# Table sums of the adaptive norms moved from columns of TensorE to row sums on VectorE, with 22 of the jobs in the plain feed-forward

## The chip, the core and the metric

The kernel runs on one core of one Trainium2 chip. The metric is the device time of one execution in microseconds (us). Engines are named TensorE (PE in the rows; PEld is its weight load), VectorE (DVE), ScalarE (ACT), GpSimd (POOL) and SyncE (SP, whose queue issues the DMAs).

## What is computed

One inference step of a network of two layers over 640 tokens (512 latent tokens and 128 prompt tokens) with 1024 features. Each layer is a gated feed-forward at half weight, a block of attention and recurrent mixers, and a second gated feed-forward. In front of each of the three stands an RMS norm whose scale, shift and gate come from a condition vector. There are two conditions, one for each group of tokens:

```python
def modulate(x, shift, scale):
    return x * (1 + scale) + shift

def adaln_params(cond, w_ada, b_ada):
    m = jax.nn.silu(cond) @ w_ada + b_ada
    return jnp.split(m[:, None, :], N_MOD, axis=-1)

def swiglu(h, w1, w2):
    gate, up = jnp.split(h @ w1, 2, axis=-1)
    return (jax.nn.silu(gate) * up) @ w2
...
        mod_ctx = adaln_params(c_ctx[None, :], w_ada[l], b_ada[l])
        mod_lat = adaln_params(c, w_ada[l], b_ada[l])
```

`w_ada` is 1024 x 9216 in each layer, 37.7 MB in float32. Its product with the two condition vectors is cut into 18 jobs for each layer, 36 in all; one job makes 512 outputs for both conditions from 2 MB of the table.

## The kernel before

Activations are kept transposed, features on the 128 partitions and tokens along the row (two halves of 320). Every large product is done in three TensorE passes: a float32 operand is split into a high part (a copy on ScalarE) and a remainder (a subtraction on VectorE, or on GpSimd), by `split` (L76); the weights go through `load` and `parts` (L80, L86) with six buffers for raw tiles and four for split ones. `linear` and `products` (L96 to L118) issue the matmuls.

The stages in order are: a start (L1256 to L1267) that makes the tables of the first norm and the first sums of squares; layer 0's first feed-forward, which is **plain** (no sums of weight blocks, all 22 blocks of hidden units at 96 matmuls); layer 0's mixer; its second feed-forward; then layer 1's feed-forward, mixer and feed-forward. The last three feed-forwards are plain in three blocks and use a scheme with seven products of sums of quarter blocks in the other 19 (`block`, L335), with extra sums on VectorE and GpSimd. A feed-forward goes through four passes of 5, 5, 6 and 6 blocks; each pass ends with eight products with `w2` that are added into `x` (L198). The mixer ends in attention over eight heads (`mla`, L1169 on) and the output product with `wo` (L667 to L677).

A job of the tables is `adaln(l, i)` (L375). In the start it is eight loads of 256 KB and eight TensorE matmuls with the condition as the two weight columns (L387), a copy of the 2 x 512 result (L409), four transposes (L412) and an addition of the bias (L417). Elsewhere (L389 to L407) the eight tiles are scaled and summed on the engines with features of the input on the partitions: two first products on ScalarE (L396), fourteen multiply-adds of 128 x 512 on VectorE (L398), then each of the two sums is split (a copy on ScalarE, a subtraction on GpSimd, tile `adah`), four TensorE matmuls with columns of ones add over the partitions (L407), and L409, L412 and L417 follow as in the start. The table tiles (`adaw`) have three buffers here, twelve in the start.

`plan` (L434) cuts each job into five steps and gives each a weight; `fill(weight, ...)` (L425) is called in the loops (12.4 after a block, 0.9 times the pass's size after each `w2` product, 1.5 in attention, 2.3 after a `wo` product) and issues the steps that have come due; `flush` issues the rest. By this plan jobs 0 to 3 are in the start, 18 in layer 0's first feed-forward, 4 in its second, 5 in layer 1's first feed-forward and 5 in layer 1's mixer (its attention heads and `wo` products). Layer 0's mixer and layer 1's second feed-forward have none. Within this order a compile-time scheduler places each engine's instructions by priority and by its own estimate of when they are ready; on the chip each engine and each queue then runs in the order so fixed.

Of the kernel before, what the change touches and what calls it, by code (L numbers as in the profile page):

```python
# [16 lines left out]
KD = 8  # L17
# [26 lines left out]
class Net:  # L44
# [193 lines left out]
    def ffn(self, w1, w2, A, B, G, plain=PLAIN):  # L238


        nc = self.nc
        tt = nc.vector.tensor_tensor
        with self.pool("ffn") as fp, self.banks(L=6, G=2):
            self.adap = fp
            low = lambda tag, bufs: fp.tile([P, 2, 320], F32, tag=tag, name=self.nm(tag), bufs=bufs)
            first = [self.weight(w, KD, P) for w in (w1[0], w1[NJ])]
            h, sums = self.combos(fp, A, B, plain < NJ)
            j = 0
            for size in PASSES:
                mid = []  # L250
                for _ in range(size):
                    sg = low("sg", 2)
                    if j < plain:
                        for n, w in enumerate((w1[j], w1[NJ + j])):
                            w = first[n] if j == 0 else self.weight(w, KD, P)
                            for c in range(2):
                                p = self.pt("L")[:, :320]
                                self.products(p, w, h[c])
                                if n == 0:
                                    i1 = nc.scalar.activation(sg[:, c], p, AF.Silu)  # L260
                                else:
# [110 lines left out]
        return self.modnorm(_Bufs(pool, dict(hf=3)), A, B)  # L372


    def adaln(self, l, i, start=False):  # L375


        nc, a, mod = self.nc, self.a, self.mods[l]
        ap = self.adap
        ps = None  # L380
        if start:
            kind = "G"
            ps = self.pt(kind)
            for q in range(KD):
                raw = ap.tile([P, 512], F32, tag="adaw", name=self.nm("adaw"), bufs=12)
                nc.sync.dma_start(raw, a['wada'][l, i, q])
                nc.tensor.matmul(ps[:2, :], lhsT=self.cs[:, q, :], rhs=raw, start=(q == 0), stop=(q == KD - 1))  # L387
        else:
            acc = [ap.tile([P, 512], F32, tag=t, name=self.nm(t), bufs=1) for t in ("ada0", "ada1")]  # L389
            for q in range(KD):  # L390
                raw = ap.tile([P, 512], F32, tag="adaw", name=self.nm("adaw"), bufs=3)
                nc.sync.dma_start(raw, a['wada'][l, i, q])
# [8 lines left out]
            kind = "G" if "G" in self.psb else "T"  # L401
            ps = self.pt(kind)
            for g in range(2):
                hi, lo = (ap.tile([P, 512], F32R, tag="adah", name=self.nm("adah"), bufs=2) for _ in range(2))
                self.split(acc[g], hi, lo, True)
                for n, x in enumerate((hi, lo)):
                    nc.tensor.matmul(ps[:2, :], lhsT=self.sel[:, g, :], rhs=x, start=(g + n == 0), stop=(g + n == 2))  # L407
        row = ap.tile([2, 512], F32, tag="adah", name=self.nm("adarow"), bufs=2)
        nc.scalar.activation(row, ps[:2, :], AF.Copy)  # L409
        ps = self.pt(kind)  # L410
        for q in range(4):
            nc.tensor.transpose(ps[:, q * 2:q * 2 + 2], row[:, q * P:(q + 1) * P], self.ident[:2, :2])  # L412
        pv = ps[:, :8].rearrange("p (q c) -> p q c", c=2)
# [51 lines left out]
    def mixer(self, l, A, B, G):  # L465
# [8 lines left out]
            h = self.modnorm_in(mp, A, B)  # L474
        self.close_x()
        gp = self.gpool = self.enter("gdn")
        st = self.enter("stage")
        stage = lambda s=None: st.tile([P, T], F32, tag="stg", name=self.nm("stg"), bufs=3)

# [164 lines left out]
        self.mla(l, range(2), hook=lambda: list(t))  # L644
        self.leave()
        with self.pool("wo") as wp:
            self.adap = wp
            o = {}

            def osplit(i, f):  # L650
# [16 lines left out]
            with self.banks(L=6, G=2):  # L667
                order = (8, 9, 10, 11, 4, 5, 6, 7, 0, 1, 2, 3)
                for n in range(KD):
                    w = self.weight(a['wo'][l, n, :, 8:], 4, P) + self.weight(a['wo'][l, n, :, :8], 8, P)  # L670
                    w = w[:4] + w[8:] + w[4:8]
                    if n < KD - 1:
                        i = self.residual(n, w, [o[i] for i in order], G, True)
                        self.fill(2.3, i, i)
                    else:
                        self.flush()
                        self.closing([n], [w], [o[i] for i in order], G)  # L677

    def hp_open(self):
# [394 lines left out]
    def pv(self, blocks, vv, o, r0, c0, width):  # L1074
# [25 lines left out]
        return nc.scalar.activation(o[r0:r0 + 64, c0:c0 + width], po[r0:r0 + 64, :width], AF.Copy)  # L1100

    def swa(self, l):
        nc, att = self.nc, self.att
# [63 lines left out]
    def mla(self, l, heads, wp=None, osplit=None, hook=None):  # L1167
        nc, a, att = self.nc, self.a, self.att
        for head in heads:  # L1169
# [25 lines left out]
            for pair in range(2):  # L1195
                prs = [fin(n, 0, 2, 320) for n in (2 * pair, 2 * pair + 1)]
                blocks = [(s, [(prs[j], s * P, j) for j in range(2)]) for s in range(5)]
                i = self.pv(blocks, vv, ot, r0, pair * 256, 256)
            if wp:
                self.fill(1.5, i, i)  # L1200
# [19 lines left out]
    def body(self):  # L1220
# [14 lines left out]
        sel = ct("sel", [P, 2, 2])  # L1235
        nc.vector.memset(sel, 0.0)
        for g in range(2):
            nc.vector.memset(sel[:, g, g:g + 1], 1.0)
        self.sel = ct("selr", [P, 2, 2], F32R)
        self.hi(self.sel, sel)  # L1240
# [13 lines left out]
        self.hp_open()  # L1254
        self.open_x()
        with self.pool("ada") as self.adap, self.banks(G=2, N=1):  # L1256
            for i in (0, 2, 1, 3):
# [27 lines left out]
        self.bd = [ct(f"bd{i}", [P, 512]) for i in range(4)]  # L1285
        for b in self.bd:
            nc.gpsimd.memset(b, 0.0)
# [4 lines left out]
        ffn, mix = 22 * 12.4 + 0.9 * 165, 6 * 1.5 + 7 * 2.3  # L1292
        for l in range(L):
            mods = lambda j: (self.A[l][j], self.mods[l][:, 3 * j], self.G[l][j])
            if l == 0:
                self.plan((jobs[4:6], 58), (jobs[6:22], ffn - 58))
            else:
                self.plan((jobs[26:31], ffn))
            self.ffn(a['w1a'][l], a['w2a'][l], *mods(0), NJ if l == 0 else PLAIN)
            self.plan((((), jobs[31:36])[l], mix))  # L1300
            self.mixer(l, *mods(1))
            self.plan(((jobs[22:26], ())[l], ffn))
            self.ffn(a['w1b'][l], a['w2b'][l], *mods(2))
        with self.pool("fin") as fp, self.banks(G=4):
            for j, p in enumerate((self.r[0], self.spread(self.r[1], 1, WINDOWS[1]))):
# [64 lines left out]
def _layout(x):  # L1370
# [22 lines left out]
    out['wada'] = C(x['w_ada'].reshape(L, KD, P, 18, 512).transpose(0, 3, 1, 2, 4))  # L1393
# [40 lines left out]
```

## Time and profile before

| | us |
|---|---|
| median of 3 runs | 3305.92 (3305.45 to 3310.22) |
| the profiled execution | 3302.95 |
| its span, first to last instruction | 3301.2 |
| mean granted TensorE clock | 0.979 of full speed |
| busy: TensorE, VectorE, ScalarE, GpSimd | 3182.5, 2383.2, 1559.5, 985.9 |

The span is what the profile covers; the execution's own time is 1.75 us more. Busy times are unions, so overlapping matmuls count once. A row of a group of instructions gives line, engine, operation, output and input tiles, shapes, count, busy time, mean duration, and the engine's idle time in front of them with what ended it. The "chain" is the sequence of work that is followed back from the last instruction of a stretch.

### The profile page before, as it was taken

The page shows a single profiled execution, that of the slowest core. Times are in us where ns is not written, and L with a number is a line of the kernel's source. Part 1 is how long each engine was busy: PE and PEld are TensorE (multiplying, and loading weights), DVE is VectorE, ACT ScalarE, POOL GpSimd, SP SyncE. Part 2 cuts the span into 40 slices and gives each one's busy share as a digit, 9 for nine tenths or more (in the row PEclk, how much of TensorE's full clock was granted, in tenths as well). Part 3 has the DMA queues.
Part 4 walks back from the last instruction along what each step waited for, and adds up shares of the span by engine and source line. Part 5 has one row for each costly group of instructions (what it writes and reads, how often), then busy time and mean ns, then how long its engine had stood idle before and what let it go on. Part 6 is the DMA issues. An engine that isn't in the chain of part 4 may idle for free.

```text
span 3301.2 us, 58370 instructions
## 1 busy us (share of the span) xinstructions
PE 3182.5 (96%) x21400; PEld 3053.1 (92%) x21400; DVE 2383.2 (72%) x5137; ACT 1559.5 (47%) x3453; POOL 985.9 (30%) x846
## 2 busy tenths in 40 slices
PE   8999999999998999999999999999998989899998
PEld 5999999999987899999999999999997869899998
DVE  4767767787886447887877897777778656766875
ACT  3333334645666544433453343465466664533433
POOL 0111101221343303553434464222114331233541
PEclk9999998999999999999999999999999989999999
DMA  6445544332534322333223333323244255222222
GB/s 221 144 140 164 158 142 139 96 99 85 171 90 115 97 75 90 97 102 106 89 85 100 106 98 101 117 86 110 73 158 123 69 150 157 77 74 84 77 90 68
DMA packets 234352, 364.90 MB, mean 111 GB/s; under 512 B 34129, under 2 KB 82385, under 8 KB 234065
## 3 DMA queue, kind: packets, MB, share of 16 engines
q1 hardware_dynamic: 234064, 361.17, 35.6%
q8 instruction: 168, 2.75, 0.3%
q14 instruction: 120, 0.98, 0.1%
HBM read 315.03 MB, written 46.04 MB: 109 GB/s over the span
## 4 chain that ended last, share of the span: by engine, by line
PE 79%; DVE 9%; ACT 4%; issue 3%; DMA 2%; POOL 2%; SPq 0%; POOLq 0%; ACTq 0%; DVEq 0%
PE psL L114 35%; PE psL L101 29%; PE psT L1098 3%; PE psG L859 2%; DVE wlo L78 2%; PE psT L1087 1%; PE psS L1192 1%; PE psS L898 1%; DVE ada L398 1%; PE psS L901 1%; PE psG L407 1%; DMA of<-do 1%; PE psS L1137 1%; DMA adaw<-in_wada_dram 1%; ACT pr L1066 1%
## 5 line engine op out<-in xcount | busy, mean ns | idle before, releaser
L69 ACT ACTIVATE whi<-wr 128x512 fp32r<-128x512 f32 (+3 forms) x733 | 417.7, 578 | 680.6 <-PE psL L114 407.3
L114 PE MATMUL psL<-mid,whi 128*128 128x320 f32 x2816 | 629.9, 311 | 0.0
L78 DVE TENSOR_TENSOR wlo<-wr,whi 128x512 fp32r<-128x512 f32 (+2 forms) x619 | 428.6, 699 | 244.6 <-ACT whi L69 243.4
L114 PEld LDWEIGHTS psL<-mid,whi 128*128 128x128 f32 x2816 | 474.7, 189 | 4.1 <-issue 0.5
L114 PE MATMUL psL<-mid,wlo 128*128 128x320 f32 x1408 | 435.2, 310 | 1.0 <-DVE wlo L78 1.0
L398 DVE SCALAR_TENSOR_TENSOR ada<-adaw,cs,ada 128x512 f32<-128x512 f32 x448 | 341.3, 794 | 24.3 <-ACT ada L396 17.5
L101 PE MATMUL psL<-hx,whi 128*128 128x320 f32 x1368 | 339.7, 310 | 0.0
L198 DVE SCALAR_TENSOR_TENSOR x<-psL,G,x 128x320 f32<-128x320 f32 (+2 forms) x432 | 173.1, 435 | 167.1 <-PE psL L114 166.5
L78 POOL TENSOR_TENSOR adah<-ada,adah 128x512 fp32r<-128x512 f32 x64 | 94.7, 1480 | 648.1 <-ACT adah L69 507.1
L114 PEld LDWEIGHTS psL<-mid,wlo 128*128 128x128 f32 x1408 | 265.3, 189 | 2.8 <-DVE wlo L78 1.3
L78 DVE TENSOR_TENSOR wlo<-ws,whi 128x512 fp32r<-128x512 f32 x228 | 241.0, 1060 | 29.2 <-ACT whi L69 28.4
L101 PE MATMUL psL<-ha,whi 128*128 128x320 f32 x952 | 237.0, 317 | 9.8 <-DVE ha L309 8.5
L101 PEld LDWEIGHTS psL<-hx,whi 128*128 128x128 f32 x1368 | 239.3, 188 | 0.6
L101 PE MATMUL psL<-hc,whi 128*128 128x320 f32 x952 | 236.6, 310 | 3.0 <-ACT hc L308 3.0
L101 PE MATMUL psL<-hb,whi 128*128 128x320 f32 x952 | 230.8, 310 | 0.0
L101 PE MATMUL psL<-hd,whi 128*128 128x320 f32 x808 | 229.4, 310 | 0.0
L1071 POOL TENSOR_TENSOR pr<-pr,den 128x640 f32<-128x640 f32 (+3 forms) x160 | 153.8, 968 | 231.1 <-DVE den L1070 173.7
L69 ACT ACTIVATE whi<-ws 128x512 fp32r<-128x512 f32 x228 | 142.1, 628 | 164.5 <-PE psL L101 123.5
L101 PE MATMUL psL<-hx,wlo 128*128 128x320 f32 x684 | 212.1, 310 | 0.0
L352 POOL TENSOR_TENSOR ws<-wr,wr 128x512 f32<-128x512 f32 x57 | 84.6, 1484 | 389.9 <-DMA wr<-in_w1b_dram 185.8
L78 POOL TENSOR_TENSOR wlo<-wr,whi 128x512 fp32r<-128x512 f32 x114 | 167.3, 1477 | 81.6 <-ACT whi L69 61.7
L1098 PE MATMUL psT<-pt,vv 128*128 128x256 f32 (+1 forms) x640 | 163.4, 381 | 17.2 <-ACT pt L1094 16.5
(361 smaller groups left out, 8355.9 us busy)
## 6 DMA issues: line engine op xcount, KB each, us to landing
adaw<-in_wada_dram SPq DMA_DIRECT2D x288, 256.0 KB, 2.8
wr<-in_w1a_dram SPq DMA_DIRECT2D x176, 256.0 KB, 2.9
wr<-in_w1b_dram SPq DMA_DIRECT2D x176, 256.0 KB, 2.9
wr<-in_win_dram SPq DMA_DIRECT2D x108, 256.0 KB, 2.8
wr<-in_w2a_dram SPq DMA_DIRECT2D x64, 256.0 KB, 2.7
wr<-in_w2b_dram SPq DMA_DIRECT2D x64, 256.0 KB, 2.7
wr<-in_wo_dram SPq DMA_DIRECT2D x48, 256.0 KB, 2.8
dqn<-hd SPq DMA_DIRECT2D x24, 320.0 KB, 2.3
```

The lines of the kernel that those rows point to most:

```text
L69: self.nc.scalar.activation(dst, src, AF.Copy)
L78: (self.nc.gpsimd if gpsimd else self.nc.vector).tensor_tensor(lo, src, hi.bitcast(F32), ALU.subtract)
L101: self.nc.tensor.matmul(p, lhsT=w, rhs=r, start=(first and k + n == 0), stop=(last and k == kt - 1 and n == 2))
L114: i = nc.tensor.matmul(p[:m, :cw], lhsT=w[:, :m], rhs=r[:, c0:c0 + cw], start=(k == 0 and n == 0), stop=(k == kt - 1 and n == 2))
L198: i = self.nc.vector.scalar_tensor_tensor(xs, ps[j][:, c0:c0 + n], G[:, k, g:g + 1], xs, ALU.mult, ALU.add)
L352: pt(s1, a21, a22, ALU.add)
L398: nc.vector.scalar_tensor_tensor(acc[g], raw, c, acc[g], ALU.mult, ALU.add)
L407: nc.tensor.matmul(ps[:2, :], lhsT=self.sel[:, g, :], rhs=x, start=(g + n == 0), stop=(g + n == 2))
L859: nc.tensor.matmul(p[:, s], lhsT=lhs[:, s], rhs=rhs[:, s], start=True, stop=True)
L898: nc.tensor.matmul(p1[:, :P], lhsT=qw[:, u, c, 64 * d:64 * d + P], rhs=S, start=True, stop=True)
L1071: nc.gpsimd.tensor_tensor(pr, pr, den[:, 0:1].to_broadcast([P, w]), ALU.mult)
L1098: nc.tensor.matmul(po[:, oc:oc + w], lhsT=vv[:, vb, :], rhs=hl[ti][:, s0:s0 + w], start=(n == 0), stop=(n == len(place) - 1))
```

## The change

A job outside the first two (0 and 2, which stay on TensorE) now takes the table transposed: 128 output features on the partitions and the 1024 input features along the row. For each of four tiles of 128 x 1024 (512 KB, two buffers) and each condition, one VectorE instruction multiplies the tile with the condition (SiLU applied, copied to all partitions, tile `crow`, 1 MB) and writes the row's sum through `accum_out`. The sum already has the features on partitions, so the split, the matmuls with ones, the copy and the transposes fall away. `conditions` loads `crow` and applies SiLU on ScalarE, once in the start and once in each feed-forward that has jobs.

```diff
+            if self.job:
+                self.conditions()
...
+    def conditions(self):
+
+        self.crow = self.adap.tile([P, 2, D], F32, tag="crow", name=self.nm("crow"), bufs=1)
+        self.nc.sync.dma_start(self.crow, self.a['crow'].unsqueeze(0).to_broadcast([P, 2, D]))
+        for g in range(2):
+            self.nc.scalar.activation(self.crow[:, g], self.crow[:, g], AF.Silu)
+
...
-            acc = [ap.tile([P, 512], F32, tag=t, name=self.nm(t), bufs=1) for t in ("ada0", "ada1")]
-            for q in range(KD):
-                raw = ap.tile([P, 512], F32, tag="adaw", name=self.nm("adaw"), bufs=3)
-                nc.sync.dma_start(raw, a['wada'][l, i, q])
+            pv = ap.tile([P, 4, 2], F32, tag="adac", name=self.nm("adac"), bufs=2)
+            for q in range(4):
+                raw = ap.tile([P, D], F32, tag="adat", name=self.nm("adat"), bufs=2)
+                nc.sync.dma_start(raw, a['wadat'][l, i * 4 + q])
                 for g in range(2):
-                    c = self.cs[:, q, g:g + 1]
-                    if q == 0:
-                        nc.scalar.activation(acc[g], raw, AF.Copy, scale=c)
-                    else:
-                        nc.vector.scalar_tensor_tensor(acc[g], raw, c, acc[g], ALU.mult, ALU.add)
-                if q % 2:
-                    yield
...
+                    out = raw if g else ap.tile([P, D], BF16, tag="adas", name=self.nm("adas"), bufs=1)
+                    nc.vector.scalar_tensor_tensor(out, raw, 1.0, self.crow[:, g], ALU.mult, ALU.mult, accum_out=pv[:, q, g:g + 1])
+                yield
```

The plan changes too: 22 jobs in layer 0's first feed-forward, 5 in its second, 5 in layer 1's first, none in a mixer, and in the start jobs 1 and 3 take the new way.

```diff
             for i in (0, 2, 1, 3):
-                list(self.adaln(0, i, start=True))
+                list(self.adaln(0, i, start=i % 2 == 0))
...
-                self.plan((jobs[4:6], 58), (jobs[6:22], ffn - 58))
+                self.plan((jobs[4:6], 58), (jobs[6:26], ffn - 58))
             else:
-                self.plan((jobs[26:31], ffn))
+                self.plan((jobs[31:], ffn))
             self.ffn(a['w1a'][l], a['w2a'][l], *mods(0), NJ if l == 0 else PLAIN)
-            self.plan((((), jobs[31:36])[l], mix))
             self.mixer(l, *mods(1))
-            self.plan(((jobs[22:26], ())[l], ffn))
+            self.plan(((jobs[26:31], ())[l], ffn))
```

The calls of `fill` and `flush` in the mixer are removed. The four zeroed tiles `bd` of the recurrent mixer, made once before (L1285), are now made and zeroed at the start of each mixer, and the columns of ones (`sel`) are gone.

## Rows read from the trace of the kernel before

**Rows 1.** The page: busy time by engine, and the chain that ended last
```profile
PE 3182.5 (96%) x21400; PEld 3053.1 (92%) x21400; DVE 2383.2 (72%) x5137; ACT 1559.5 (47%) x3453; POOL 985.9 (30%) x846
PE 79%; DVE 9%; ACT 4%; issue 3%; DMA 2%; POOL 2%; SPq 0%; POOLq 0%; ACTq 0%; DVEq 0%
```

**Rows 2.** Timeline, ScalarE: the norm row that closes each feed-forward and mixer
```profile
551.80 0.44 ACT L227 ACTIVATE rn<-psG 128x320 f32<-128x320 f32 x1 [0.64 <-PE psG L163]
...
1220.55 0.44 ACT L227 ACTIVATE rn<-psG 128x320 f32<-128x320 f32 x1 [1.31 <-PE psG L163]
...
1677.93 0.44 ACT L227 ACTIVATE rn<-psG 128x320 f32<-128x320 f32 x1 [0.39 <-PE psG L163]
...
2144.27 0.44 ACT L227 ACTIVATE rn<-psG 128x320 f32<-128x320 f32 x1 [1.11 <-PE psG L163]
...
2839.58 0.44 ACT L227 ACTIVATE rn<-psG 128x320 f32<-128x320 f32 x1 [2.36 <-PE psG L163]
...
3285.54 0.44 ACT L227 ACTIVATE rn<-psG 128x320 f32<-128x320 f32 x1 [0.40 <-PE psG L163]
```

**Rows 3.** Busy time by stretch: length, then busy time and count of each engine
```profile
core 0: us, PE busy (x) PEld busy (x) DVE busy (x) ACT busy (x) POOL busy (x), PEclk, DMA share, GB/s
...
63.00:545.00 482.00, 479.83 (x3237) 467.50 (x3235) 339.85 (x592) 174.46 (x318) 53.21 (x36) 1.00 0.50 152
...
1216.00:1241.00 25.00, 20.23 (x125) 19.14 (x123) 21.52 (x56) 21.14 (x52) 3.93 (x4) 0.86 0.19 64
...
1700.00:2136.00 436.00, 428.64 (x2869) 420.39 (x2868) 357.39 (x561) 179.17 (x342) 195.02 (x130) 1.00 0.34 105
```

**Rows 4.** The chain by line in 63 to 545 us, the plain feed-forward
```profile
by line: PE psL L101 62.7%; PE psL L114 32.0%; PE psG L407 3.4%; PE psG L412 1.3%; POOL adah L78 0.3%; ACT adah L69 0.1%; ACT adarow L409 0.1%; issue 0.1%; ACTq L69 0.0%
```

**Rows 5.** Groups by line and shape: VectorE's multiply-adds, a one-column instruction, ScalarE's accumulator read
```profile
L398 DVE SCALAR_TENSOR_TENSOR ada<-adaw,cs,ada 128x512 f32<-128x512 f32 x252 | 182.8, 755 | 21.2 <-ACT ada L396 17.5 <-DMA adaw<-in_wada_dram 3.4
...
L307 DVE SCALAR_TENSOR_TENSOR mid<-x,A,rn 128x320 f32<-128x320 f32 x32 | 15.1, 547 | 0.0
...
L1070 DVE RECIPROCAL den<-den 128x1 f32<-128x1 f32 x160 | 25.4, 159 | 48.2 <-ACT pr L1066 46.8
...
L1066 ACT ACTIVATION_READ_ACCUMULATOR pr<-psS,nb,rq 128x1 f32 x80 | 16.2, 202 | 0.0
```

**Rows 6.** Timeline of VectorE at 147 us: two multiply-adds in a row
```profile
147.31 1.41 DVE L398 SCALAR_TENSOR_TENSOR ada<-adaw,cs,ada 128x512 f32<-128x512 f32 x2
```

**Rows 7.** Busy time of line 398 alone in two later stretches
```profile
1241.00:1680.00 439.00, 43.13 (x56) 1.00 0.31 96
1700.00:2136.00 436.00, 64.66 (x70) 1.00 0.34 105
```

**Rows 8.** The chain by line in layer 1's mixer: attention, 2640 to 2740, and `wo`
```profile
by line: PE psT L1098 24.7%; PE psS L1192 12.4%; PE psT L1087 10.6%; DMA of<-do 8.9%; issue 8.3%; DVE ada L398 5.8%; POOL pr L1071 5.8%; DVE mx L1061 4.2%; DMA adaw<-in_wada_dram 3.7%; ACT pr L1066 3.4%; ACT pt L1094 2.8%; POOL adah L78 2.5
...
by line: PE psL L114 86.3%; PE psG L407 3.4%; PE psG L145 2.8%; POOL adah L78 2.7%; PE psG L412 1.5%; ACT adah L69 1.3%; issue 0.8%; PE psT L1098 0.7%; ACT adarow L409 0.6%; ACT whi L69 0.1%; POOLq L78 0.0%; ACTq L69 0.0%
```

**Rows 9.** The start: timeline of VectorE and TensorE, and DMA to 60 us
```profile
44.80 0.17 DVE L417 TENSOR_TENSOR mod<-psG,small 128x8 f32<-128x8 f32 x1 [7.26 <-PE psG L412]
...
50.82 0.64 PE L101 MATMUL psL<-hc,whi 128*128 128x320 f32 x1 [2.98 <-ACT hc L308]
...
17.28 4.46 SPq L386 DMA_DIRECT2D adaw<-in_wada_dram  x6
...
GB/s 0 66 284 351 366 354 396 400 397 388 393 394 398 394 392 385 389 321 319 361 380 386 376 391 392 388 388 351 368 175 7 5 0 0 0 0 0 0 0 0
...
adaw<-in_wada_dram SPq DMA_DIRECT2D x35, 256.0 KB, 5.4
```

**Rows 10.** DMA in 63 to 545 us: issues, KB, us to landing; SP's waits
```profile
adaw<-in_wada_dram SPq DMA_DIRECT2D x141, 256.0 KB, 2.8
...
dx<-x SPq DMA_DIRECT2D x6, 320.0 KB, 3.5
...
SPq L392 <- DVE ada L398: 102.0, 107, 2.1
```

**Rows 11.** GpSimd's zeroing of the `bd` tiles
```profile
L1287 POOL MEMSET bd<- x4: 524/524/524, 0.7 to 2.1; 128x512 f32 x4
```

More of the change, by code (lines that the diff above doesn't have):

```diff
@@ L379, in adaln @@
         ap = self.adap
-        ps = None
         if start:
-            kind = "G"
-            ps = self.pt(kind)
+            ps = self.pt("G")
             for q in range(KD):
                 raw = ap.tile([P, 512], F32, tag="adaw", name=self.nm("adaw"), bufs=12)
-                nc.sync.dma_start(raw, a['wada'][l, i, q])
+                nc.sync.dma_start(raw, a['wada'][i // 2, q])
                 nc.tensor.matmul(ps[:2, :], lhsT=self.cs[:, q, :], rhs=raw, start=(q == 0), stop=(q == KD - 1))
-        else:
-            acc = [ap.tile([P, 512], F32, tag=t, name=self.nm(t), bufs=1) for t in ("ada0", "ada1")]
-            for q in range(KD):
-                raw = ap.tile([P, 512], F32, tag="adaw", name=self.nm("adaw"), bufs=3)
-                nc.sync.dma_start(raw, a['wada'][l, i, q])
+            row = ap.tile([2, 512], F32, tag="adarow", name=self.nm("adarow"), bufs=1)
@@ new lines, in adaln @@
+            nc.scalar.activation(row, ps[:2, :], AF.Copy)
+            ps = self.pt("G")
+            for q in range(4):
+                nc.tensor.transpose(ps[:, q * 2:q * 2 + 2], row[:, q * P:(q + 1) * P], self.ident[:2, :2])
+            pv = ps[:, :8].rearrange("p (q c) -> p q c", c=2)
+        else:
+            pv = ap.tile([P, 4, 2], F32, tag="adac", name=self.nm("adac"), bufs=2)
+            for q in range(4):
+                raw = ap.tile([P, D], F32, tag="adat", name=self.nm("adat"), bufs=2)
+                nc.sync.dma_start(raw, a['wadat'][l, i * 4 + q])
@@ L393, in adaln @@
                 for g in range(2):
-                    c = self.cs[:, q, g:g + 1]
-                    if q == 0:
-                        nc.scalar.activation(acc[g], raw, AF.Copy, scale=c)
-                    else:
-                        nc.vector.scalar_tensor_tensor(acc[g], raw, c, acc[g], ALU.mult, ALU.add)
-                if q % 2:
-                    yield
[L401 to L413, printed above, removed]
+                    out = raw if g else ap.tile([P, D], BF16, tag="adas", name=self.nm("adas"), bufs=1)
+                    nc.vector.scalar_tensor_tensor(out, raw, 1.0, self.crow[:, g], ALU.mult, ALU.mult, accum_out=pv[:, q, g:g + 1])
@@ L476, in mixer @@
         gp = self.gpool = self.enter("gdn")
+        self.bd = [gp.tile([P, 512], F32, name=self.nm("bd")) for i in range(4)]
+        for b in self.bd:
+            nc.gpsimd.memset(b, 0.0)
         st = self.enter("stage")
@@ L646, in mixer @@
         with self.pool("wo") as wp:
-            self.adap = wp
             o = {}
@@ L672, in mixer @@
                     if n < KD - 1:
-                        i = self.residual(n, w, [o[i] for i in order], G, True)
-                        self.fill(2.3, i, i)
+                        self.residual(n, w, [o[i] for i in order], G, True)
                     else:
-                        self.flush()
                         self.closing([n], [w], [o[i] for i in order], G)
@@ L1099, in pv @@
                              start=(n == 0), stop=(n == len(place) - 1))
-        return nc.scalar.activation(o[r0:r0 + 64, c0:c0 + width], po[r0:r0 + 64, :width], AF.Copy)
+        nc.scalar.activation(o[r0:r0 + 64, c0:c0 + width], po[r0:r0 + 64, :width], AF.Copy)
     def swa(self, l):
@@ L1197, in mla @@
                 blocks = [(s, [(prs[j], s * P, j) for j in range(2)]) for s in range(5)]
-                i = self.pv(blocks, vv, ot, r0, pair * 256, 256)
-            if wp:
-                self.fill(1.5, i, i)
+                self.pv(blocks, vv, ot, r0, pair * 256, 256)
             self.pv([(5, [(fin(4, T, 1, P), 0, 0)])], vv, ot, r0, TL, P)
@@ L1234, in body @@
         nc.vector.memset(self.ones, 1.0)
[L1235 to L1240, printed above, removed]
         self.mhalf = ct("mhalf", [P, 8])
@@ L1256, in body @@
         with self.pool("ada") as self.adap, self.banks(G=2, N=1):
+            self.conditions()
             for i in (0, 2, 1, 3):
-                list(self.adaln(0, i, start=True))
+                list(self.adaln(0, i, start=i % 2 == 0))
                 if i == 2:
@@ L1284, in body @@
         self.sh8 = [i ^ 8 for i in range(32)]
-        self.bd = [ct(f"bd{i}", [P, 512]) for i in range(4)]
-        for b in self.bd:
-            nc.gpsimd.memset(b, 0.0)
         self.nsink = ct("nsink", [P, 2 * 8])
@@ L1291, in body @@
         jobs = [(l, i) for l in range(L) for i in range(18)]
-        ffn, mix = 22 * 12.4 + 0.9 * 165, 6 * 1.5 + 7 * 2.3
+        ffn = 22 * 12.4 + 0.9 * 165
         for l in range(L):
@@ L1392, in _layout @@
     out['wo'] = tiles(x['w_out'], 12, P)
-    out['wada'] = C(x['w_ada'].reshape(L, KD, P, 18, 512).transpose(0, 3, 1, 2, 4))
+    out['wada'] = C(x['w_ada'][0].reshape(KD, P, 18, 512).transpose(2, 0, 1, 3)[0:4:2])
+    out['wadat'] = C(x['w_ada'].transpose(0, 2, 1).reshape(L, 72, P, D))
+    out['crow'] = C(np.stack([x['c'][0], x['c_ctx']]))
     fp = lambda v: v.reshape(L, -1, P).transpose(0, 2, 1)
```

## The prediction

> **What bounds the kernel now.** First the page: TensorE is busy for 96% of the span and holds 79% of the chain that ended last, VectorE holds 9% [rows 1]. So an edit pays where it takes TensorE work off the chain or ends a wait of TensorE, and costs where VectorE comes late. A mean over stages with different limits says no more than that, so next come the stages. The norm row that closes each of them marks its end [rows 2]: layer 0's mixer lasts 1220.55 - 551.80 = 668.8 us, its second feed-forward 457.4, layer 1's first feed-forward 466.3, its mixer 695.3, its second feed-forward 446.0. The last three feed-forwards do the same products, with 4, 5 and 0 jobs of the tables in them; the mixers are alike too, with 0 and 5. These differences are the price of the jobs as they stand: 11.4 us for 4, 20.4 for 5, and 26.5 for the 5 in the mixer.
>
> In the plain feed-forward, 63 to 545 us, TensorE is busy for 479.83 of 482 us and VectorE for 339.85, or 71% [rows 3]. Its chain is TensorE almost throughout, and the parts that belong to the tables (L407, L412, and waits for `adah` and `adarow`) are 3.4 + 1.3 + 0.3 + 0.1 + 0.1 = 5.2% [rows 4], or 25.1 us for 18 jobs: 1.4 us a job.
>
> **The change, part by part.** *TensorE's share of a job.* The four matmuls with ones, the transposes and the waits for their operands vanish. At 1.4 us a job this is 25.1 us in the plain feed-forward, whose added jobs then cost TensorE nothing, 5.6 us in layer 0's second feed-forward and 7.0 in layer 1's first.
>
> *VectorE's share.* Fourteen instructions of 755 ns go [rows 5]. Eight of 128 x 1024 come. From 320 columns at 547 ns to 512 at 755 a column costs 1.08 ns, so 1024 should take 755 + 512 x 1.08 = 1.31 us. Two in a row take 1.41 us, 0.05 each less than alone [rows 6], so 1.26. No VectorE row of this kernel has an accumulator output. On ScalarE, reading the accumulator is an instruction of its own, of 202 ns, and VectorE's one-column instruction takes 159 [rows 5]. The bounds are 0 and 0.20 us; I take 0.12, the one-column row less some overlap. A sum is then about 1.38 us and a job 11.0 us of VectorE, against 182.8 / 18 = 10.2 now. On VectorE the new way is thus no cheaper at all.
>
> The Trainium skill ("VectorE: DVE Perf Modes", "Two Vector instructions with no wait between them") says that a VectorE operation which also writes out its accumulator is two instructions, the main one and an accumulator read, and this speaks against the change. The same page's fit for float32 pairs, (N + 151)/0.96 ns, under "The TRN2 errata", gives an estimate of 1.22 us for the main one; with it a job would be 10.7 us. No run shown here has such a VectorE instruction.
>
> *22 jobs for 18 in the plain feed-forward.* Its other VectorE work is 339.85 - 182.8 = 157 us; the jobs become 22 x 11.0 = 242. That is 399 us in a stretch of 457 (482 less 25), or 87%. The bounds of what the crowding costs: nothing, as the chain shows at 71%; or what layer 1's first feed-forward pays at 357.39 of 436 us, 82% [rows 3], where 20.4 - 7.0 = 13.4 us are waits. Those blocks depend more on VectorE than the plain ones, so I take 8 us. Net -17.
>
> *Layer 0's second feed-forward, 5 jobs for 4.* TensorE -5.6. The waits (11.4 - 5.6 = 5.8 us) stay and grow with VectorE's job time, from 43.13 us [rows 7] to 55 or more: +2. The condition row needs two SiLUs of 1024 columns on ScalarE; they come ahead of the norm's work in a changeover where ScalarE is busy for 21.14 of 25 us [rows 3], so up to 2.4 us of them shows: +1.6. Net -2. *Layer 1's first feed-forward, 5 for 5.* TensorE -7.0; VectorE 64.66 us [rows 7] against some 60; ScalarE and GpSimd lose their part, -3 of the waits; the SiLUs +2. Net -8.
>
> *Layer 1's mixer.* All five jobs leave. If it becomes like layer 0's, 26.5 us go. The chain bears it out: in attention, `ada`, `adaw` and `adah` together hold 5.8 + 3.7 + 2.5 = 12% of 100 us, and in `wo` the tables hold 3.4 + 2.7 + 1.5 + 1.3 + 0.6 = 9.5% of 95 us [rows 8]: 21 us named, the rest in issue and queues. I take -26. The four memsets of 524 ns in each mixer [rows 11] run on GpSimd while the input products begin and nothing needs it: 0; uncovered, 2 us each.
>
> *The start.* The loads run near 390 GB/s until 44 us [rows 9]; `crow` adds 1 MB, 2.7 us. Jobs 1 and 3 now wait on VectorE. Their loads begin to be issued at 17.3 us [rows 9]; with `crow` ahead and 5.4 us to land, the first sum starts near 25, and sixteen of them end at 47 if none waits. With two buffers each of the last six loads can be issued only when a tile is done: (5.4 + 2.8) / 2 = 4.1 us a tile against 2.8 of work, up to 8 us more. The bounds are therefore +2 and +10 on the last table addition, now at 44.80, behind which the steady products start at 50.82 [rows 9]. I take +8, as the queue is full there.
>
> **Sum**: -17 - 2 - 8 - 26 + 8 = -45 us against the profiled execution's 3302.95: 3258. The median of the runs is 3.0 us above that execution, so 3261.
>
> **The rivals.** *The cover holds.* VectorE's added work fits into its idle time, GpSimd's and ScalarE's relief shortens more waits in the two later feed-forwards, and the start loses 3 us: -25 - 5 - 12 - 26 + 3 = -65, or 3241. For it: 47 us of VectorE's 142 idle us in the plain feed-forward would be enough. Against it: 87% leaves little play for a queue in fixed order.
>
> *VectorE becomes the bound in the plain feed-forward.* If a sum takes 1.65 us, 157 + 22 x 8 x 1.65 = 447 us of 457: the 25 us are given back whole, and the later feed-forwards gain nothing: -26 + 8 = -18, or 3288. For it: the accumulator's price is not in these rows. Against it: the read would have to take 0.39 us, three times my term and twice ScalarE's.
>
> *Slower: the table loads hold up VectorE's queue.* With two buffers the load of a tile is issued only when the tile two before is done. A load of 256 KB lands in 2.8 us, one of 320 KB in 3.5 [rows 10]; 512 KB should take 3.5 to 5.6. If steps run back to back, the 2.8 us of the tile between cover only part, and VectorE stands for w us in front of each of the 88 tiles, with the weight remainders and sums of the products behind it. The plain feed-forward then takes 399 + 88 w. The other stages give 28 us, so from w = (482 + 28 - 399) / 88 = 1.26 us the kernel is slower; at 1.5 it takes 3303 + 21 + 3 = 3327. For it: `fill` issues three or four steps at once, and SP already waits 102 us for VectorE to free table tiles [rows 10]. Against it: on average a tile has 457 / 88 = 5.2 us, and now VectorE waits only 3.4 us for `adaw` in this stretch [rows 5].
>
> *The mixer's 26.5 us are not the jobs'.* If only the `wo` part goes, it is 13 less: 3274.
>
> **How the numbers follow.** Forecast (3247 to 3274) 0.47; cover holds (3226 to 3247) 0.20; VectorE the bound (3274 to 3299) 0.17; mixer 0.07; loads hold the queue (3299 and more) 0.09. A measurement of this kernel tells about 0.2%, 6.6 us, from no change. Slower by more than that needs w above 1.3 us: 0.07. Within it: 0.06, the edges of the two unfavourable cases. Faster: 0.87. The range leaves out the slow case and the lowest end: 3228 to 3296.
>
> **What would show it.** Right: no psG matmul in 63 to 545; that stretch's products in about 465 us with VectorE near 87%; layer 1's mixer within 3 us of layer 0's; rows of the sums near 1.26 us with an accumulator read of about 0.12 to 0.2; the first steady product at 55 to 61 us. Wrong: VectorE waiting for `adat` by more than 0.7 us a tile; a sum above 1.6 us; TensorE waiting for VectorE's weight remainders (L78) in the plain feed-forward by more than 20 us; a mixer that stays near 695.

## The result and the profile after

The changed kernel takes 3233.56 us (median of 4 runs, 3228.27 to 3235.18) against 3305.68 before (4 runs): a ratio of 0.9784, 95% interval 0.9769 to 0.9799, or 72 us less. The forecast was 3261, its range 3228 to 3296, and the rival "the cover holds" stood at 3241. The direction, the range and the main mechanism were right; the gain is 1.6 times the one forecast, near the lower edge of the range, and nearer to that rival.

The page's busy times and the shares of its last chain, after (answering to [rows 1]):

```profile
PE 3102.4 (96%) x21104; PEld 3006.9 (93%) x21104; DVE 2389.2 (74%) x5230; ACT 1471.1 (45%) x3297; POOL 902.6 (28%) x786
PE 74%; DVE 14%; ACT 4%; issue 4%; DMA 3%; POOL 1%; SPq 0%; POOLq 0%; DVEq 0%; ACTq 0%
```

TensorE, ScalarE and GpSimd lose 80, 88 and 83 us of work. VectorE gains 6: two more jobs are on it, and a job's sums have become hardly cheaper there, but all that stood around them is gone. VectorE's share of the chain has grown from 9% to 14%.

The norm row that closes each stage, after (answering to [rows 2]):

```profile
533.24 0.44 ACT L227 ACTIVATE rn<-psG 128x320 f32<-128x320 f32 x1 [1.48 <-PE psG L163]
...
1197.80 0.44 ACT L227 ACTIVATE rn<-psG 128x320 f32<-128x320 f32 x1 [1.31 <-PE psG L163]
...
1654.38 0.44 ACT L227 ACTIVATE rn<-psG 128x320 f32<-128x320 f32 x1 [0.39 <-PE psG L163]
...
2109.16 0.44 ACT L227 ACTIVATE rn<-psG 128x320 f32<-128x320 f32 x1 [0.39 <-PE psG L163]
...
2772.88 0.44 ACT L227 ACTIVATE rn<-psG 128x320 f32<-128x320 f32 x1 [1.31 <-PE psG L163]
...
3218.12 0.44 ACT L227 ACTIVATE rn<-psG 128x320 f32<-128x320 f32 x1 [0.39 <-PE psG L163]
```

The differences of these marks, and the first product from which TensorE runs on steadily (50.82 us before, 63.01 after), divide the 67.8 us by which the profiled span is shorter:

| stretch | before | after | change | forecast |
|---|---|---|---|---|
| start, to the first steady product | 50.8 | 63.0 | +12.2 | +8 |
| plain feed-forward, layer 0 | 501.0 | 470.2 | -30.8 | -17 |
| mixer, layer 0 | 668.8 | 664.6 | -4.2 | 0 |
| second feed-forward, layer 0 | 457.4 | 456.6 | -0.8 | -2 |
| first feed-forward, layer 1 | 466.3 | 454.8 | -11.6 | -8 |
| mixer, layer 1 | 695.3 | 663.7 | -31.6 | -26 |
| the rest | 461.6 | 460.5 | -1.1 | 0 |

The new sums (line 408), their accumulator reads, and VectorE's waits for their tiles, over the whole kernel:

```profile
L408 DVE SCALAR_TENSOR_TENSOR adas<-adat,crow x136: 1207/1217/2209, 27.0 to 2086.8; 128x1024 bf16<-128x1024 f32 x136
L408 DVE DVE_READ_ACCUMULATOR adas<-adat,crow x136: 74/81/86, 28.1 to 2087.9; 128x1 f32 x136
...
  DMA adat<-in_wadat_dram: 11.8, 18
...
DMA to landing us min/median/max: 3.3/3.7/7.6
```
```profile
26.99 1.23 DVE L408 SCALAR_TENSOR_TENSOR adas<-adat,crow 128x1024 bf16<-128x1024 f32 x1 [1.12 <-DMA adat<-in_wadat_dram]
28.14 0.08 DVE L408 DVE_READ_ACCUMULATOR adas<-adat,crow 128x1 f32 x1
```

The three figures behind a count are minimum, median and maximum in ns. A sum takes 1.217 us and its accumulator read 0.081. The Trainium skill ("VectorE: DVE Perf Modes", "Two Vector instructions with no wait between them") says that such an operation is two instructions; this trace agrees, and prices the second at 0.08 us. In the timeline (the second view, with start and duration) the read begins at 28.14 us, before the sum's row ends at 26.99 + 1.23 = 28.22, so it adds next to nothing to the 1.22. A load of 512 KB lands in 3.7 us, and VectorE waits for one 18 times, 11.8 us in all.

In the plain feed-forward TensorE does nothing but products now. These are busy times of all engines from 75 to 520 us, busy time of line 408 alone over the stage, and the chain by line in 75 to 520 (answering to [rows 3, 4]):

```profile
75.00:520.00 445.00, 445.00 (x3037) 445.00 (x3036) 352.42 (x680) 118.98 (x224) 0.00 (x0) 1.00 0.58 178
```
```profile
63.00:533.24 470.24, 213.43 (x352) 0.99 0.56 174
```
```profile
by line: PE psL L101 67.4%; PE psL L114 25.3%; issue 1.4%; DVE adat L408 1.2%; DMA adat<-in_wadat_dram 1.1%; DVE adas L408 1.0%; DVE wlo L78 1.0%; DVE x L198 0.9%; DVE sq L132 0.7%; DVE mid L78 0.2%; DVE G L419 0.0%; DVE mod L413 0.0%; DVEq
```

TensorE is busy for 445.00 of 445 us, and VectorE (third figure) for 352.42, 79%. The 176 sums with their reads take 213.43 us, 1.21 each, or 9.7 us a job in place of 10.2.

The start has grown longer. On VectorE the last table addition is at 53.37 us in place of 44.80, and then a load of masks holds the queue; on ScalarE a second SiLU of the condition row stands among the norm's instructions; on TensorE the steady products begin (answering to [rows 9]):

```profile
53.37 0.17 DVE L413 TENSOR_TENSOR mod<-adac,small 128x8 f32<-128x8 f32 x1
53.57 0.17 DVE L417 SCALAR_TENSOR_TENSOR A<-mod,small 128x8 f32<-128x8 f32 x1
56.09 0.23 DVE L1266 CAST bmaskf<-mk 128x128 bf16<-128x128 f32 x1 [2.35 <-DMA mk<-in_masks_dram]
```
```profile
61.31 2.00 ACT L382 ACTIVATE crow<-crow 128x1024 f32<-128x1024 f32 x2 [0.29 <-DMA crow<-in_crow_dram]
```
```profile
63.01 0.90 PE L101 MATMUL psL<-ha,whi 128*128 128x320 f32 x2 [4.28 <-DVE ha L311]
```

One thing in the kernel before was not read closely enough ahead of the forecast. This is its chain at the end of the plain feed-forward (start, duration, what), and busy times of all engines over the same end; the first figure behind the last count is the granted clock:

```profile
541.50 0.64 ACT adah L69
...
542.21 1.27 POOL adah L78
...
543.53 0.41 PE psG L407
...
543.96 0.59 ACT adarow L409
...
545.00 3.94 PE psG L145 x18
```
```profile
540.00:545.00 5.00, 2.83 (x17) 1.58 (x16) 0.15 (x1) 1.69 (x3) 2.07 (x2) 0.99 0.17 52
545.00:552.00 7.00, 6.83 (x30) 6.43 (x30) 1.85 (x6) 1.30 (x3) 0.85 (x1) 0.50 0.08 29
552.00:560.00 8.00, 8.00 (x36) 7.44 (x35) 6.49 (x15) 4.70 (x10) 1.09 (x1) 0.50 0.60 200
```

The last job's copy, subtraction and matmuls follow one another in front of the closing sums (L145). TensorE is idle for 2.2 us of the 5 from 540 to 545, and then its granted clock is 0.50, the 1.2 GHz level, for 15 us. This is the price of a job that comes due late more than of the old way of summing: with earlier steps it goes (an experiment below), and the changed kernel has a smaller stop at the same place, with the clock at 0.72 behind it:

```profile
531.65 1.55 PE L163 MATMUL psG<-mats,rs 128*128 128x128 f32 x6 [1.30 <-POOL rs L150]
```
```profile
533.24:541.00 7.76, 6.94 (x38) 5.68 (x37) 6.17 (x15) 4.57 (x9) 0.81 (x1) 0.72 0.44 146
```

### The profile page after: what moved, and what is told of

Its sections match the earlier page's. It is cut to its first block, busy times and chain, and to the rows that moved or that the text cites. A ratio compares the mean times of both kernels' runs of the same rounds, so it can differ in the third digit from the quotient of the medians.

```text
span 3233.4 us, 57261 instructions
## 1 busy us (share of the span) xinstructions
PE 3102.4 (96%) x21104; PEld 3006.9 (93%) x21104; DVE 2389.2 (74%) x5230; ACT 1471.1 (45%) x3297; POOL 902.6 (28%) x786
## 4 chain that ended last, share of the span: by engine, by line
PE 74%; DVE 14%; ACT 4%; issue 4%; DMA 3%; POOL 1%; SPq 0%; POOLq 0%; DVEq 0%; ACTq 0%
PE psL L114 34%; PE psL L101 25%; PE psT L1094 3%; DVE wlo L78 3%; PE psG L855 3%; PE psS L1188 1%; PE psT L1083 1%; DVE adas L408 1%; PE psS L894 1%; DVE adat L408 1%; DMA of<-do 1%; PE psS L897 1%; DMA adat<-in_wadat_dram 1%; ACT pr L1062 1%; DVE tsum L353 1%
## 5 line engine op out<-in xcount | busy, mean ns | idle before, releaser
L78 DVE TENSOR_TENSOR wlo<-wr,whi 128x512 fp32r<-128x512 f32 (+2 forms) x619 | 416.5, 680 | 216.6 <-ACT whi L69 213.5
L150 POOL TENSOR_TENSOR rs<-rs,mhalf 128x3 f32<-128x3 f32 (+1 forms) x18 | 19.8, 1099 | 920.9 <-DVE rs L149 892.9
L78 DVE TENSOR_TENSOR wlo<-ws,whi 128x512 fp32r<-128x512 f32 x228 | 256.5, 1130 | 20.9 <-ACT whi L69 20.7
L101 PEld LDWEIGHTS psL<-ha,whi 128*128 128x128 f32 x952 | 167.9, 192 | 33.7 <-ACT ha L310 19.1
L408 DVE SCALAR_TENSOR_TENSOR adas<-adat,crow 128x1024 bf16<-128x1024 f32 x136 | 169.1, 1243 | 11.9 <-DMA adat<-in_wadat_dram 11.8
```

Source lines behind the costliest of these rows:

```text
L78: (self.nc.gpsimd if gpsimd else self.nc.vector).tensor_tensor(lo, src, hi.bitcast(F32), ALU.subtract)
L101: self.nc.tensor.matmul(p, lhsT=w, rhs=r, start=(first and k + n == 0), stop=(last and k == kt - 1 and n == 2))
L408: nc.vector.scalar_tensor_tensor(out, raw, 1.0, self.crow[:, g], ALU.mult, ALU.mult, accum_out=pv[:, q, g:g + 1])
```

## The experiments

### The plan alone

The kernel before, its jobs spread as in the change:

```diff
-                self.plan((jobs[4:6], 58), (jobs[6:22], ffn - 58))
+                self.plan((jobs[4:6], 58), (jobs[6:26], ffn - 58))
...
-                self.plan((jobs[26:31], ffn))
+                self.plan((jobs[31:], ffn))
...
-            self.plan((((), jobs[31:36])[l], mix))
...
-            self.plan(((jobs[22:26], ())[l], ffn))
+            self.plan(((jobs[26:31], ())[l], ffn))
```

> The old way of summing (VectorE sums over features on partitions, TensorE adds over partitions) with the new plan of 22, 5, 5 and 0 jobs. If way and plan each have their own part: layer 1's mixer falls from 695 to about 665 us, the plain feed-forward grows by 4 jobs of 1.4 us of TensorE, layer 0's second feed-forward by 3: about 3283 us, a third of the whole gain. If the plan alone were the cause of the gain: about 3235. If the way alone were: no change, 3303.

Measured: 3284.39 us, a ratio of 0.9926 (0.9907 to 0.9945), as the first case expected. Layer 1's mixer lies between these two marks:

```profile
2157.68 0.44 ACT L227 ACTIVATE rn<-psG 128x320 f32<-128x320 f32 x1 [0.60 <-PE psG L163]
...
2821.76 0.44 ACT L227 ACTIVATE rn<-psG 128x320 f32<-128x320 f32 x1 [1.31 <-PE psG L163]
```

It takes 664.1 us: without old jobs it loses 31 of its 695. The plain feed-forward gives 11 of them back (563.71 - 51.49 = 512.2 against 501.0), 2.8 us for each of the four added jobs. That is not what a job costs as it goes along: at 1.4 us of TensorE four jobs are 5.6, and about as much is a longer stop at the stage's end. There TensorE waits for the last job's sums, 7.8 us in four pieces (5.48, twice 0.81, 0.68) against 2.2 in three in the kernel before:

```profile
551.61 0.59 PE L407 MATMUL psG<-adah,selr 128*2 128x512 f32 x1 [5.48 <-ACT adah L69]
```

Layer 0's second feed-forward takes 464.4 us, 7.1 more for its one added job where 3 were expected.

### The way alone

The changed kernel with the plan of before: 18, 4 and 5 jobs, and 5 as row sums in layer 1's mixer.

```diff
         with self.pool("wo") as wp:
+            self.adap = wp
+            if self.job:
+                self.conditions()
...
+                        self.fill(2.3, i, i)
...
+                        self.flush()
...
+                self.fill(1.5, i, i)
...
-                self.plan((jobs[4:6], 58), (jobs[6:26], ffn - 58))
+                self.plan((jobs[4:6], 58), (jobs[6:22], ffn - 58))
...
-                self.plan((jobs[31:], ffn))
+                self.plan((jobs[26:31], ffn))
...
+            self.plan((((), jobs[31:36])[l], mix))
             self.mixer(l, *mods(1))
-            self.plan(((jobs[26:31], ())[l], ffn))
+            self.plan(((jobs[22:26], ())[l], ffn))
```

> The row sums on VectorE with the plan of before: 18, 4, 5 jobs in feed-forwards and 5 in layer 1's mixer, two in the start. If the mixer's 26.5 us were paid for TensorE's matmuls, the copies and GpSimd's subtractions, the mixer gets them back here too and the kernel is at about 3240. If they are paid for VectorE's time and the loads among the attention's short instructions, the mixer stays above 680 us and the kernel is at 3250 to 3260.

Measured: 3229.19 us (0.9770, 0.9758 to 0.9783), below both expectations and no slower than the whole change. Layer 1's mixer with five row-sum jobs:

```profile
2098.22 0.44 ACT L227 ACTIVATE rn<-psG 128x320 f32<-128x320 f32 x1 [0.39 <-PE psG L163]
...
2767.50 0.44 ACT L227 ACTIVATE rn<-psG 128x320 f32<-128x320 f32 x1 [1.31 <-PE psG L163]
```

That is 669.3 us, 2 to 7 more than with none (661.8 to 667.7 in eight kernels whose layer 1 mixer has no jobs). So the mixer paid its 26.5 us mostly for what goes with the old way, the matmuls, the copies, ScalarE's first products and GpSimd's subtractions, and not for VectorE's time, which is much the same in both ways; which of them it was is not separated. Layer 0's second feed-forward with four jobs takes 450.1 us (456.6 with five). Moving the jobs out of the mixer, which the forecast gave 26 us, is worth nothing that can be measured beside the new way of summing: the mixer gains 5.6 and that feed-forward loses 6.5. The two halves of the change, 20 and 75 us alone, are 72 together, because each of them alone takes 26 to 31 us out of layer 1's mixer.

### The start on TensorE

```diff
-                nc.sync.dma_start(raw, a['wada'][i // 2, q])
+                nc.sync.dma_start(raw, a['wada'][i, q])
...
-            self.conditions()
             for i in (0, 2, 1, 3):
-                list(self.adaln(0, i, start=i % 2 == 0))
+                list(self.adaln(0, i, start=True))
```

> The changed kernel, with all four jobs of the start on TensorE as before and no condition row in the start. If the row sums in the start are what delays the first steady product from 50.8 to 63.0 us: that product goes back to about 51 us and the kernel to about 3222. Rival: the start is bound by its loads either way, and only 3 us come back: 3231.

Measured: 3226.26 us (0.9757, 0.9741 to 0.9773), 7 less than the change, between the expectation and the rival. The start did get 11.4 of its 12.2 us back:

```profile
51.61 0.90 PE L101 MATMUL psL<-ha,whi 128*128 128x320 f32 x2 [4.28 <-DVE ha L311]
```

But the end of the plain feed-forward got worse. A piece of its chain there, the last table tile's first sum, the closing's norm instructions on VectorE and TensorE, and busy times behind it:

```profile
513.01 4.56 DMA adat<-in_wadat_dram
```
```profile
517.60 1.23 DVE L408 SCALAR_TENSOR_TENSOR adas<-adat,crow 128x1024 bf16<-128x1024 f32 x1 [0.19 <-DMA adat<-in_wadat_dram]
...
520.02 0.15 DVE L149 TENSOR_SCALAR rs<-psG 128x3 f32<-128x3 f32 x1
...
521.15 1.65 PE L163 MATMUL psG<-mats,rs 128*128 128x128 f32 x6 [1.76 <-POOL rs L150]
```
```profile
520.00:530.00 10.00, 8.85 (x38) 8.54 (x39) 6.88 (x20) 4.39 (x10) 0.95 (x2) 0.53 0.46 141
```

The closing's norm instruction (L149) is queued on VectorE behind the two sums of the last table tile, 2.4 us of work. The 4.56 us in the chain are the time of that tile's load, from issue to landing, and not a wait: VectorE works on the tile before and on the products meanwhile, and stands only 0.19 us for the load. TensorE waits 1.76 us for the norm, and its granted clock from 520 to 530 us is 0.53. In the changed kernel the same two sums stand at 528.1 to 530.5 us, with no wait for their load (4.76 us, also in the chain), and TensorE waits 1.30.

### Steps due earlier, in the kernel before and behind the start on TensorE

```diff
-                self.plan((jobs[4:6], 58), (jobs[6:22], ffn - 58))
+                self.plan((jobs[4:6], 58), (jobs[6:22], ffn - 58 - 30))
```

> The kernel before, with the steps of the plain feed-forward's 16 later jobs due 30 units of weight earlier, so that none is left for the stage's last products. If the last job's chain (copy, subtraction, two matmuls, copy, transposes) in front of the closing sums costs a stop of TensorE of some 3 us and then 15 us at half its clock: both vanish, 5 to 8 us in the first feed-forward and the mixer behind it, 3296 to 3300. Rival: the half clock comes from the closing's own short waits and is there anyway; no change beyond 2 us.

Measured: 3295.54 us, a ratio of 0.9976 (0.9965 to 0.9987), so 9 us less, half a microsecond below the expectation. The stretch that held the half clock:

```profile
541.00:548.00 7.00, 6.37 (x49) 6.10 (x48) 2.62 (x6) 2.15 (x5) 0.85 (x1) 1.00 0.13 45
548.00:556.00 8.00, 6.79 (x42) 5.96 (x41) 6.95 (x17) 5.07 (x10) 1.10 (x1) 0.80 0.73 244
```

The clock is 1.00 through the closing and 0.80 behind it, and the feed-forward is 5.3 us shorter (495.7 against 501.0). The mixer behind it is not shorter, 668.6, so that half of the expectation fell. Of the rest, 4.1 us are in layer 1's mixer (691.2 against 695.3), which the edit does not touch: a mixer's length differs by some microseconds between traces without a cause that these runs show.

```diff
-                self.plan((jobs[4:6], 58), (jobs[6:26], ffn - 58))
+                self.plan((jobs[4:6], 58), (jobs[6:26], ffn - 58 - 40))
```

> All four jobs of the start on TensorE, and the plain feed-forward's 20 later jobs due 40 units earlier. If the last table tiles, whose loads the closing's norm instruction on VectorE stands behind, cost the wait of 4.6 us and the half clock behind it: 4 to 8 us less than with the start on TensorE alone (3226), 3218 to 3222. Rival: VectorE is the tighter in the rest of the stage, and TensorE waits there instead: 3226 or more.

Measured: 3222.97 us (0.9752, 0.9739 to 0.9764), 3 less than with the start alone, which the intervals do not tell apart. The trace does: no table sum stands in front of the closing any more, TensorE waits 0.70 us for the norm, the clock stays at 1.00, and the stage takes 469.1 us where it took 471.2. That the load's 4.6 us were a wait, as the expectation has it, is not so; the sums queued in front of the norm are enough:

```profile
515.00:522.00 7.00, 6.30 (x47) 6.03 (x47) 2.16 (x6) 2.68 (x6) 0.85 (x1) 1.00 0.23 79
522.00:530.00 8.00, 6.48 (x46) 4.83 (x44) 7.49 (x18) 4.54 (x9) 1.09 (x1) 1.00 0.65 213
```

### One and three buffers for a table tile

```diff
-                raw = ap.tile([P, D], F32, tag="adat", name=self.nm("adat"), bufs=2)
+                raw = ap.tile([P, D], F32, tag="adat", name=self.nm("adat"), bufs=1)
```

> The changed kernel with one buffer for a table tile in place of two. If the slower rival's mechanism is real and two buffers just avoid it: a tile then needs a load of 3.7 us and 2.5 us of sums one after the other, 6.2 us, where the plain feed-forward gives each of its 88 tiles 5.3 us; that stage grows from 470 to about 550 us, the start by 15, and the kernel is slower than before, 3320 to 3340. If the spacing of the steps covers the load anyway: within 15 us of 3234.

Measured: 3396.04 us, slower than before by a ratio of 1.0270 (1.0253 to 1.0287), and 56 us above the range expected. VectorE's wait in 80 to 520 us, and busy times in what should be the mixer:

```profile
DVE adas L408 <- DMA adat<-in_wadat_dram: 123.5, 57, 3.4
```
```profile
640.00:680.00 40.00, 0.00 (x0) 0.00 (x0) 15.75 (x29) 0.00 (x0) 0.00 (x0) 0.50 0.28 83
```

So the slower rival's mechanism exists: 57 waits of 2.2 us. The start takes 19 us more and the feed-forward 45, and the tiles left over run on into the mixer, where TensorE does nothing in the 40 us of this stretch; that mixer takes 757 us, 92 more than in the change, and that was not expected. Two buffers keep the waits at 7.9 us in 75 to 520 us, 14 of them.

With three buffers, behind the earlier steps:

> The same with three buffers for a table tile. If VectorE's waits for table loads (7.9 us in the plain feed-forward) still reach TensorE somewhere: 2 to 4 us less than with two. If they only use up idle time: within 2 us of it.

Measured: 3221.40 us (0.9745, 0.9732 to 0.9758) against 3222.97 with two: no difference that the intervals show. The waits for table tiles are gone from the trace, so with two they used up idle time.

### Half as much again on VectorE

The first condition's sum is made twice; nothing is left out.

```diff
-                for g in range(2):
+                for g in (0, 0, 1):
```

> The changed kernel with the first condition's sum made twice: half as much VectorE work again for the tables, nothing left out. If VectorE's idle time is what pays for the sums: in the plain feed-forward 352 + 109 us of work no longer fit into 445, so that stage grows by 20 to 40 us, the start by 10, the two later feed-forwards by 5 to 10 each: 3275 to 3300. If VectorE has play left beyond its busy time's sum (its order is fixed, so waits and not sums would decide): under 3255.

Measured: 3318.53 us, a ratio to the kernel before of 1.0037 (1.0023 to 1.0051): 85 us more than the change, 18 above the range expected. Where it falls is the surprise. Busy times of all engines, then of line 408 alone in the last two of these stretches:

```profile
80.00:500.00 420.00, 420.00 (x2866) 420.00 (x2865) 381.83 (x726) 109.92 (x202) 0.00 (x0) 1.00 0.54 161
...
540.00:560.00 20.00, 5.70 (x25) 5.22 (x24) 19.32 (x38) 1.10 (x2) 1.82 (x1) 0.50 0.62 186
560.00:580.00 20.00, 0.00 (x0) 0.00 (x0) 19.59 (x34) 0.00 (x0) 0.00 (x0) 0.50 0.41 132
```
```profile
540.00:560.00 20.00, 17.43 (x29) 0.50 0.62 186
560.00:580.00 20.00, 19.55 (x33) 0.50 0.41 132
```

With VectorE at 91% TensorE is still busy for 420.00 of 420 us, and the feed-forward is no longer than the change's (538.06 - 68.82 = 469.2). What VectorE cannot do in time is left to the end: 37 us of sums stand in front of the mixer's norm, with TensorE idle and its clock at 0.50, and that mixer takes 709 us (664.6 in the change). The two later feed-forwards take 18 us more each.

### Where the jobs should go

With the start on TensorE and steps due earlier: 22, 2, 3 jobs and 5 in layer 1's mixer with two buffers; and 26, 3, 3 and none with three. The plan of the second:

```diff
-                self.plan((jobs[4:6], 58), (jobs[6:26], ffn - 58))
+                self.plan((jobs[4:6], 58), (jobs[6:30], ffn - 58 - 40))
...
-                self.plan((jobs[31:], ffn))
+                self.plan((jobs[33:], ffn))
...
-            self.plan(((jobs[26:31], ())[l], ffn))
+            self.plan(((jobs[30:33], ())[l], ffn))
```

> Start on TensorE, steps of the plain feed-forward 40 units earlier, and the jobs spread as 22, 2, 3 and 5 in layer 1's mixer. If a row-sum job costs some 2 us in each of the two later feed-forwards and only 1 us in the mixer: against the kernel with 22, 5, 5 and 0 jobs (3223) 6 + 4 us go and 5 come, about 3216. Rival: the mixer's long row-sum instructions cost more once its attention is the only place: 3225 or more.

> Start on TensorE, three buffers, steps 40 units earlier, and 26 jobs in the plain feed-forward, 3 and 3 in the two later ones, none in a mixer. If the plain feed-forward's VectorE still has room (352 of 445 us at 22 jobs, 392 at 26): the two later feed-forwards give 2 us a job, 8 us, and the kernel is at about 3213. If fixed order makes TensorE wait before VectorE is full: the tail of table tiles reaches the closing again and the kernel is at 3222 or more.

Measured: 3219.19 us (0.9733, 0.9714 to 0.9751) and 3216.05 us (0.9729, 0.9711 to 0.9748), each some 3 above what was expected, and not told apart. Both beat the change by 14 to 18 us, of which the start on TensorE and the earlier steps, alone 3222.97 (0.9739 to 0.9764), are 11; from that kernel the intervals tell neither apart. In the second, from 60 to 500 us of the plain feed-forward:

```profile
60.00:500.00 440.00, 440.00 (x3002) 440.00 (x3002) 391.76 (x768) 118.15 (x221) 0.00 (x0) 1.00 0.66 197
```

VectorE is at 89% with 26 jobs, TensorE loses nothing, and the later feed-forwards take 449.8 and 449.9 us with three jobs each, where five cost 456.6 and 454.8 in the change. The traces also show why the total gains less: against the kernel with 22, 5, 5 and 0 jobs the two later feed-forwards are 10.5 us shorter, but the two mixers, which have no jobs in either, 6.9 longer. In the first of the two kernels the later feed-forwards gain 12.0 and the mixers give back 9.8.

## Why the prediction was right, and by how much it was off

**TensorE's share of a job** was right as a mechanism: in the plain feed-forward TensorE has nothing left but products. Its size was near too. The chain gave 1.4 us a job and 25.1 us; between the two kernels with earlier steps, which have little of a stop, the stage goes from 495.7 to 469.1 us, 26.6. What the forecast left out is the closing: the late last job cost the kernel before a stop and a spell at half the clock, 5.3 us of that stage, and the changed kernel pays 1.1 us there (470.2 against 469.1). 26.6 + 5.3 - 1.1 are the 30.8 us measured.

**The crowding of VectorE (+8)** is the step that failed: as it goes along it cost nothing. It took its price from layer 1's first feed-forward at 82%, whose blocks depend on VectorE in chains. In the plain blocks TensorE waits for nothing at 79%, at 89% with 26 jobs, or at 91% with a third sum; the stage takes 470 us each time. Crowding there is paid at the end, as a tail of table tiles in front of the closing or of the next stage: 1.1 us in the change, 44 with the third sum. The sums were also over-priced: 1.38 us forecast, 1.21 measured, as the read's 0.08 us lie almost within the sum's row, where 0.12 were added, and a column costs (1217 - 755) / 512 = 0.90 ns and not 1.08. So they take 213 us and not 242, and VectorE stands at 79% and not near 87%. The estimate of 1.22 us for the main instruction by the Trainium skill's fit ("VectorE: DVE Perf Modes", "The TRN2 errata") was the better one; the trace has 1.217.

**Layer 1's mixer (-26)** came out at -31.6, and its reason was half right. The jobs did cost that much, but they did not have to leave: with the new sums in the mixer all but 2 to 7 us of it comes back. Moving them was priced as if an old job and a new one cost the mixer the same. That the number came out near for the change is luck in so far as either half of it alone would have given it.

**The two later feed-forwards (-2 and -8)** were near, -0.8 and -11.6. Five row-sum jobs still cost 11.3 and 9.5 us there, against the 445.2 of the stage that has none, and the fifth job in the first of them is the dear one: with four it takes 450.1, with five 456.6. This is why the first of them gained so little.

**The start (+8)** measured +12.2, and the first steady product at 63.0 us lies outside the 55 to 61 given as a sign. The last table addition is 8.6 us late, as forecast, but the two buffers are only a part of the reason: VectorE's waits for the loads of the later tiles come to 2.75 us (1.57, 0.17 and 1.01 at 42.02, 44.70 and 48.21 us); the first sum begins at 26.99 and not near 25, and from 31.9 to 35.3 us weight remainders stand between the sums. What was missed is behind it: the masks' load, issued at 53.36 us, after the last sum, holds VectorE for 2.35 us. That it waits for memory which the new tiles hold is inferred from its time of issue, and was not tried by itself. The last 1.3 us lie between the first product and the steady ones (5.18 us, before 3.87), where the second SiLU of the condition row now stands on ScalarE; the kernel with the start on TensorE, which keeps that SiLU, has 5.19 there. With the four jobs on TensorE 11.4 of the 12.2 us came back.

**The rivals.** "The cover holds" described the plain feed-forward best, but had the start at +3, and its 47 us of added work do not follow from the prediction's own terms, which give 242 - 183 = 59; measured were 31. "VectorE becomes the bound" needed a sum of 1.65 us, and did not happen; the third sum shows what it would look like. "The loads hold up the queue" is real with one buffer and absent with two. "The mixer's 26.5 us are not the jobs'" is refuted by the plan alone.

**Open.** Layer 0's mixer, which has no jobs in any version, took between 661.5 and 668.8 us in the traces of kernels without a tail; its -4.2 here is not explained by the clock, as the kernel before with earlier steps shows. Moving the zeroed `bd` tiles was not tried by itself; the plan alone, which leaves them where they were, has 664.0 there, so they need not be the reason.

## What to carry to other kernels

When work is added to an engine that is off the critical path, look where its tail ends and what is queued behind that: here, with the third sum, an engine at 91% cost its main consumer nothing for 420 us, and then 44 us behind the stage's end. Before moving work out of a crowded stage, ask which of its instructions the stage pays for; making the job free of the other engines was worth 75 us, moving it 20, and both 72. Where a stage ends in a short chain over several engines, let side work come due before it.

## What was not expected of the hardware

In the kernel before, three waits of TensorE of 0.55, 0.95 and 0.68 us close together in front of the closing were followed by 15 us at a granted clock of 0.50 (the 1.2 GHz level), in which the closing's eighteen small matmuls took 3.94 us; with the steps due earlier the clock was 1.00 there and twelve and six of them took 1.23 and 0.58 us. VectorE's accumulator read took 74 to 89 ns, less than half of ScalarE's 202, and less than the one-column instruction of 159 in [rows 5]. The row sums stretched to 1.34 and 1.50 us on the mean, from 1.22, in layer 0's second feed-forward (1230 to 1650 us), where GpSimd is busy for 177.03 of 420 us; in the plain feed-forward it is busy for 0.00 of 445. That GpSimd is the reason was not tried:

```profile
L408 DVE SCALAR_TENSOR_TENSOR adat<-adat,crow 128x1024 f32<-128x1024 f32 x20 | 30.1, 1503 | 0.0
L408 DVE SCALAR_TENSOR_TENSOR adas<-adat,crow 128x1024 bf16<-128x1024 f32 x20 | 26.9, 1344 | 0.0
```
